# The causal mask's addition to the forget-gate rows: from DVE to an adding transfer of GpSimd, with another order of steps

## The chip, the cores and the metric

The kernel runs on one core of a Trainium2 chip. The metric is the device time of one launch in microseconds (us); the time before is the median of three runs. Five engines work side by side, each through its own queue in the order in which the program was written: TensorE (PE: matrix products and transposes), VectorE (DVE), ScalarE (ACT), GpSimd (POOL) and SyncE (SP, which here only starts transfers). A DMA started by SP or POOL stands in that engine's queue like any other instruction.

## What is computed

Two layers of a decoder over 512 tokens with 1024 features. Each layer has a mixing stage (three token mixers beside each other on one projection), a gated MLP and a small gated embedding stage. The part the change is about is the third mixer, attention with a forget gate, 6 heads of 64, in blocks of 128 queries:

```
c = jnp.cumsum(log_f, axis=1)                 # one row of 512 per head
s = einsum(q_i, k) * scale + c_i[..., None] - cT[:, :, None, :]
s = where(key_pos[None, :] <= q_pos[:, None], s, -inf)
out = softmax(s) @ v
```

So each score needs the key's running gate sum, and the diagonal block of 128x128 of each query block also the causal mask. The other two mixers are spatial gating (SGU) and retention (6 heads, with rotary position encoding); all three are put side by side and multiplied with `w_o`.

## The kernel before

Every instruction is first recorded by `Plan.record` and then issued in an order that `Plan.issue` (L452) works out, so all rows of the profile carry L452, and work is known by its tile. The planner models the engines, follows the order of recording as priority, and lets each stage's weight preparation run ahead of its use by a limit in the table `AHEAD` (L62). The order on each engine is therefore a result of the planner, of `AHEAD`, and of the order of steps in `STEPS` (L494): `u`, `s` are the spatial gating, `F` the attention's values and gate sums (`fox_values`, L1014), `H` the combined halves of the activations (`hT.combine`), `f0` to `f2` the query and key projections of three pairs of heads (`fox_proj`, L1052), `a0` to `a2` the attention of these pairs (`fox_attend`, L1066), `r0` to `r2`, `v`, `c0` to `c2` retention's projections, values and cores, `g`, `G`, `L` its gates. `O_ORDER` (L497) is the order in which `out_proj` (L1220) takes the eight 128-row blocks of the concatenation; blocks 5 to 7 are the three pairs of attention heads, 2 to 4 the retention.

The projections (`seven`, L860) multiply 2x2 blocks with seven products instead of eight. `seven_weights` (L837) prepares their weights: SP loads the tile `graw`, POOL starts two adding transfers into it (L847, L848), DVE makes two more sums, and ACT and DVE split each into a rounded part and a rest (`wg`, `wu`, `wsa`, `wsb`). Each exact product is three products on PE (`mm3`, L908).

In a layer the gate sums of six heads are made on PE (`cumps`, transposed as `ctps`), and written by SP as six rows to memory (`cums`). `fox_proj` takes one tile `fcb` (128x2048) for a pair of heads. For each head SP loads the row `cums`, broadcast to 128 partitions, as `cb[:, 0]`, and DVE writes `cb[:, 1]`, the same plus the mask. `fox_attend` reads `cb[:, 0]` for the blocks left of the diagonal and `cb[:, 1]` for the diagonal one, with a custom DVE instruction (`pe<-sps,fcb`) that adds the row to the scores and takes a minimum. ACT makes the exponential, DVE divides, PE transposes (`tps`, copied out as `fet` by DVE or ACT in turn), and PE multiplies with the values (`ops`), which ACT and DVE split into `cc` for `out_proj`.

Other names below: `ps<-thl,hT` are products of retention's values (`rv`, weights `traw` split into `thl`), `rm`, `rr` its rotated projections, `kps` transposes of the rotated key, `ips`, `rops`, `kvps` its core, `wo` the products of `out_proj`, `beta`, `alpha`, `gamma` the accumulators of `seven`, `hh`, `hhd`, `hT` its activations. `sps` is used by the attention scores and by the spatial gating. The mask before was a 128x128 tile in a slice of a larger tile (`mix`, L952), loaded once per layer (64 KB, L955).

Of the kernel before, what the change touches and what calls it, by code (L numbers as in the profile page):

```python
# [33 lines left out]
ALU = mybir.AluOpType  # L34
AX = mybir.AxisListType

P = 128
D = 1024
S = 512
NCH = 4  # L40
# [10 lines left out]
class Plan:  # L51
# [7 lines left out]

    SETS = {"X": 17, "W": 7}  # L60

    AHEAD = {"mix": 416, "wo": 450, "wo2": 381, "emb": 503, "gu0": 443, "gu": 478, "dn": 673, "end": 164, "pg": 300, "pg2": 392}  # L62
    LOAD = 1290
    TICK = 10240 / 3
    PHASE = 1900
# [186 lines left out]
    def issue(self):  # L252
# [41 lines left out]
        def blocked(i):  # L294
# [3 lines left out]
            for t in dict.fromkeys(ops[i][5]):  # L298
                if t not in taken:
                    tag, bufs = self.tiles[t][:2]  # L300
                    s = first[t]
                    need[tag] += 1
                    if len(slots[tag]) < need[tag] or s - front > self.AHEAD[self.stages[i]] or (s > front and live[tag][front:s].max() + need[tag] > bufs):
                        return queue(t)
# [4 lines left out]
        def queue(t):  # L309
            return f"b8 {self.kind[t]}" if t in self.kind else self.tiles[t][0]  # L310
# [160 lines left out]
def constants():  # L471
    idx = np.arange(P, dtype=np.float64)
    lg = np.log(1.0 - 2.0 ** (-5.0 - np.arange(6, dtype=np.float64)))
    diff = idx[None, :] - idx[:, None]
    decay = np.where(diff >= 0, np.exp(lg[:, None, None] * np.maximum(diff, 0.0)), 0.0) / 8.0
    qdec = np.exp(lg[:, None] * (idx + 1.0))
    kdec = np.exp(lg[:, None] * (P - 1.0 - idx)) / 8.0
    cd = np.exp(lg * P)
    hf = np.repeat(np.arange(2), 64)
    c = {}  # L480
    c["ident"] = np.eye(P)
    c["decay"] = decay.transpose(1, 0, 2).reshape(P, 6 * P)
    c["qdec"] = np.stack([qdec[2 * p + hf] for p in range(3)], 1).reshape(P, 3 * P)
    c["kdec"] = kdec.T
    c["cd"] = np.stack([cd[2 * p + hf] for p in range(3)], 1)
    c["invf"] = (10000.0 ** (-np.arange(32, dtype=np.float64) / 32))[np.arange(P) % 32][:, None]
    c["cum"] = np.concatenate([(idx[:, None] <= idx[None, :]).astype(np.float64), np.ones((P, P))], 1)
    c["mask"] = np.where(idx[None, :] <= idx[:, None], 0.0, 1e30)
    return {k: np.ascontiguousarray(v.astype(np.float32)) for k, v in c.items()}

PAIRS = [(c + p * P, d + p * P) for c, d in ((C_RQ, C_RK), (C_FK, C_FQ)) for p in range(3)] + [(C_RG, C_RG + P)]
STEPS = "u F H f0 g f1 r0 a0 v a1 G L s r1 r2 c0 f2 c1 c2 a2"  # L494
O_CHUNKS = (0, 2, 1, 3)
EARLY = {0: 0}
O_ORDER = (5, 6, 0, 1, 2, 3, 4, 7)  # L497
IDLE = 16
SUMS_BY_DMA = True
SEVEN = ("hb11", "hb21", "hh6", "hhd", "hh7", "hb22", "hh4")  # L500
# [2 lines left out]
def packed(w):  # L503

    def rows(m, order=None):

        m = m.reshape(-1, P, m.shape[-1])
        return (m if order is None else m[list(order)]).transpose(1, 0, 2)
# [16 lines left out]
    r["dn"] = [m.reshape(8, 4, P, 2, 512).transpose(0, 3, 2, 1, 4) for m in w["w_down"]]  # L525
    r["wo"] = [np.stack([rows(m[:, c:c + 512], O_ORDER) for c in (0, 512)]) for m in w["w_o"]]
    r["pg"] = [np.stack([rows(m[:, c:c + 512]) for c in (0, 512)]) for m in w["w_ple_gate"]]
# [4 lines left out]
def body(ctx, tc, a, out):  # L532
    nc = tc.nc
    plan = Plan(tc)
    V, A, G, T, SY = (plan.engine(n, e) for n, e in (
        ("DVE", nc.vector), ("ACT", nc.scalar), ("POOL", nc.gpsimd), ("PE", nc.tensor), ("SP", nc.sync)))
# [16 lines left out]
    def bank(name="ps"):  # L553
        return ppt([P, 512], F32, tag="ps", name=name, bufs=8)

    def wk(name, shape=(P, 512), dt=F32):
        return kpt(list(shape), dt, tag="wk", name=name, bufs=12)

    def b8(name, shape, dt=F32):
        kind = "W" if name in ("wg", "wsa", "wsb") else "X" if dt == F32R else None  # L560
        return b8t([P] + list(shape), dt, name, kind)
# [4 lines left out]
    def dram(name, shape):  # L566
        return dpt(list(shape), F32, tag=name, name=name, bufs=1)
# [96 lines left out]
    def v4(ps):  # L664
        return ps.rearrange("p (k t) -> p k t", k=4)
# [194 lines left out]
    def seven(h, ws, gs, us, scale=1.0, between=None):  # L860

        wg, wu, sa, sb = ws
        be, al, ga = (bank(n)[:, 0:256] for n in ("beta", "alpha", "gamma"))
        t1, t2 = slice(0, 256), slice(256, 512)

        def product(ps, w, n, first, last, part=range(4)):
            for k in part:
                ks = slice(k * P, k * P + P)
                mm3(ps, lambda i: w[i][:, ks], lambda i: h.part(n, i, k), first and k == 0, last and k == 3, True)

        def part(t, i):
            return [t[:, j, i * 512:i * 512 + 512] for j in range(2)]
        product(be, part(wg, 0), "b11", True, False)
        A.copy(gs[:, t1], be)
        product(al, part(wg, 1), "b21", True, True)
        V.tensor_tensor(out=gs[:, t1], in0=al, in1=gs[:, t1], op=ALU.add)
        product(be, part(sa, 0), "h6", False, False)
        A.copy(gs[:, t2], be)
        product(ga, part(sa, 1), "hd", True, False)
        if scale == 1.0:  # L880
            A.copy(us[:, t2], ga)
        else:
            A.mul(us[:, t2], ga, -scale)
        product(be, part(sb, 0), "h7", False, False)
        V.scalar_tensor_tensor(out=us[:, t2], in0=be, scalar=-scale, in1=us[:, t2], op0=ALU.mult, op1=ALU.subtract if scale == 1.0 else ALU.add)
        product(ga, part(sb, 1), "b22", False, True)
        V.tensor_tensor(out=gs[:, t2], in0=ga, in1=gs[:, t2], op=ALU.add)
        rest = between() if between else None
        product(be, wu, "h4", False, True, range(1) if rest else range(4))
        if rest:  # L890
            rest()
            product(be, wu, "h4", False, True, range(1, 4))
        A.mul(us[:, t1], be, -scale)
# [25 lines left out]
    def tm_chunk_major(act, u, n, done, order=range(KB), chunks=range(NCH)):  # L919
        for c in chunks:  # L920
            ps = bank()
            for j, k in enumerate(order):
                tm_mm(ps[:, 0:n], act, k, c, u, j == 0, j == KB - 1, 0, n, j)
            done(c, ps)
# [13 lines left out]
    cums = [[dram(f"cums{l}_{h}", (1, S)) for h in range(6)] for l in range(DEPTH)]  # L938


    def mixers(l, hT, uv, ready):
        plan.stage = "mix"
        m1, m2, m3, m4, m5, m6 = (b8(f"mix{i}", (2048,)) for i in range(6))
# [5 lines left out]
        au = m4[:, 0:1024].rearrange("p (c n) -> p c n", c=NCH)  # L949
        av = m4[:, 1024:2048].rearrange("p (c n) -> p c n", c=NCH)  # L950
        cst = m5[0:6, 0:512]
        mask = m5[:, 512:640]  # L952
        cosT = m5[:, 1536:2048]
        decay, qdec, cum, sinT = m6[:, 0:768], m6[:, 768:1152], m6[:, 1152:1408], m6[:, 1408:1920]
        for t, n in ((decay, "decay"), (qdec, "qdec"), (cum, "cum"), (mask, "mask")):  # L955
            SY.dma_start(out=t, in_=a["c_" + n])
        if l:
            SY.dma_start(out=sinT, in_=trig[:, 0, :])
# [93 lines left out]
        def fox_proj(p):  # L1052


            k, q = wk("fqk"), wk("fqk")
            seven(hT, seven_weights(a["w_fm"][l, 3 + p]), k, q, -0.125)
            tiles = [q, k]
            both = b8("fcb", (4, S))
            for s in range(2):
                cb = both[:, 2 * s:2 * s + 2, :]  # L1060
                SY.dma_start(out=cb[:, 0, :], in_=cums[l][2 * p + s].to_broadcast([P, S]))
                V.tensor_tensor(out=v4(cb[:, 1, :]), in0=v4(cb[:, 0, :]), in1=mask.unsqueeze(1).to_broadcast([P, NCH, P]), op=ALU.add)
                tiles.append(cb)
            return tiles

# [113 lines left out]
        fq, rq = {}, {}  # L1179
        for step in STEPS.split():  # L1180
            h = int(step[1]) if len(step) > 1 else 0
# [38 lines left out]
    def out_proj(l, cc, ready, x, new, g, nxt):  # L1220
# [4 lines left out]
        first = [bank("wo0") for _ in range(NCH)]  # L1225
        for j, k in enumerate(O_ORDER):
            for c in range(NCH):
# [18 lines left out]
        seen = []  # L1246
        tm_chunk_major(cc, u, 512, done, O_ORDER, O_CHUNKS)
        return emb
# [209 lines left out]
    g = Gains(None, ("mix_pre_g", 0))  # L1458
# [33 lines left out]
    for l in range(DEPTH):  # L1492
        ready = {}
        cc = mixers(l, hT, uv, ready)
        g = Gains(("mix_post_g", l), ("ffn_pre_g", l))
        hs = Seven(g)
        emb = out_proj(l, cc, ready, Rows(src), xd[3 * l], g, hs)
        g = Gains(("ffn_post_g", l), ("ple_pre_g", l))
        hT = Plain(g)
        ffn(l, hs, emb, ready, Rows(xd[3 * l]), xd[3 * l + 1], g, hT)  # L1500
        last = l + 1 == DEPTH
        g = Gains(("ple_post_g", l), None if last else ("mix_pre_g", l + 1))
        if last:
            ple(l, hT, Rows(xd[3 * l + 1]), ov, g, None)
        else:
            nxt = Mixed(g)
            ple(l, hT, Rows(xd[3 * l + 1]), xd[3 * l + 2], g, nxt)
            hT, src = nxt, xd[3 * l + 2]
            uv = tm_units(a["w_uv"][l + 1], 512)
# [24 lines left out]
```

## Time and profile before

| | us |
| --- | --- |
| runs, median of 3 | 1566.68 (1566.16 to 1568.85) |
| profiled execution | 1566.79 |
| its span in the profile | 1564.8 |
| PE busy | 1546.8 (99%) |
| DVE busy | 1219.5 (78%) |
| ACT busy | 888.6 (57%) |
| POOL busy | 193.3 (12%) |

The granted clock of PE was 0.998 of full speed. In a row of the timeline the first number is the start from the beginning of the span, the second the time to the modelled end of the last instruction merged into it, and a bracket gives the idle time of the engine just before and what ended it. Because PE's instructions are pipelined, the ends of one row and the start of the next overlap; the time of a run of products is best read from start to start. From the timeline, the mixing stage of layer 0 runs from about 44 to 215 us of the span and that of layer 1 from about 745 to 985; MLP and embedding fill the rest.

### The profile page before, as it was taken

What the parts mean: (1) busy time and instruction counts of PE and PEld (TensorE: products, weight loads), DVE (VectorE), ACT (ScalarE), POOL (GpSimd) and SP (SyncE); (2) the same over time, 40 slices, a digit from 0 to 9 for tenths busy, and PEclk for the clock granted to TensorE, in tenths of its full rate; (3) what the DMA queues carried; (4) which work ended last, traced back from release to release, by engine and by line L of the source; (5) the groups of instructions that cost most, each with busy time, mean ns of one, the idle gap of its engine ahead of it and who ended that gap; (6) DMA issues with size and microseconds to landing.
All of it is one profiled execution on the core that took longest, in us unless ns stands there. A gap on an engine that the chain in (4) does not pass through costs nothing.

```text
span 1564.8 us, 26898 instructions
## 1 busy us (share of the span) xinstructions
PE 1546.8 (99%) x10554; PEld 1401.3 (90%) x10554; DVE 1219.5 (78%) x2036; ACT 888.6 (57%) x1501; POOL 193.3 (12%) x233
## 2 busy tenths in 40 slices
PE   9999999999999999999999999999999999999997
PEld 6998878999899999998889898799999999999986
DVE  6778978977778778767796789799677788687685
ACT  8556647765554545535584576586555455455362
POOL 1111112101101111000120101121101011011010
PEclk9999999999999999999999999999999999999999
DMA  9444529545637446456474346295546455455641
GB/s 331 92 123 104 180 90 291 134 121 142 169 81 198 137 96 176 130 156 247 155 216 102 85 122 210 76 301 136 145 112 155 143 136 147 128 150 148 232 158 54
DMA packets 87877, 239.00 MB, mean 153 GB/s; under 512 B 10036, under 2 KB 18364, under 8 KB 87752
## 3 DMA queue, kind: packets, MB, share of 16 engines
q1 hardware_dynamic: 64856, 195.81, 36.0%
q0 software_dynamic: 22464, 40.90, 16.4%
q8 instruction: 82, 1.34, 0.3%
q10 hardware_dynamic: 432, 0.59, 0.1%
q14 instruction: 43, 0.35, 0.1%
HBM read 219.94 MB, written 17.33 MB: 152 GB/s over the span
## 4 chain that ended last, share of the span: by engine, by line
PE 91%; ACT 3%; DMA 3%; DVE 2%; issue 1%; SPq 0%; POOLq 0%; POOL 0%; DVEq 0%; ACTq 0%
PE beta L452 26%; PE dn L452 21%; PE ps L452 14%; PE gamma L452 13%; PE alpha L452 6%; PE wo L452 3%; DMA graw<-in_w_gu_dram 2%; PE hps L452 1%; PE sps L452 1%; PE tps L452 1%; PE ops L452 1%; PE eps L452 1%; PE gps L452 1%; ACT thl L452 1%; PE rops L452 1%
## 5 line engine op out<-in xcount | busy, mean ns | idle before, releaser
L452 PE MATMUL dn<-thl,act 128*128 128x512 f32 x1536 | 370.5, 391 | 0.0
L452 PEld LDWEIGHTS dn<-thl,act 128*128 128x128 f32 x1536 | 280.4, 188 | 52.3
L452 PE MATMUL ps<-thl,hT 128*128 128x512 f32 (+3 forms) x984 | 209.7, 368 | 1.1 <-ACT hT L452 0.9
L452 POOL DMA_DIRECT2D graw<-in_w_gu_dram x128 | 112.4, 917 | 759.0 <-DVE wg L452 162.2
L452 PEld LDWEIGHTS ps<-thl,hT 128*128 128x128 f32 x984 | 175.1, 188 | 25.0 <-ACT hT L452 1.5
L452 DVE TENSOR_TENSOR thl<-traw,thl 128x1024 fp32r<-128x1024 f32 (+3 forms) x124 | 142.3, 1155 | 19.3 <-ACT thl L452 19.2
L452 ACT CAST thl<-traw 128x1024 fp32r<-128x1024 f32 (+3 forms) x124 | 121.3, 995 | 22.0 <-DVE wsb L452 8.9
L452 PEld LDWEIGHTS beta<-hh,wu 128*128 128x128 f32 x936 | 125.6, 188 | 9.1
L452 PE MATMUL beta<-hh,wu 128*128 128x256 f32 x936 | 130.2, 279 | 0.0
L452 PE MATMUL beta<-hh,wsa 128*128 128x256 f32 x936 | 122.0, 279 | 1.2 <-ACT gs L452 0.8
L452 PE MATMUL beta<-hh,wsb 128*128 128x256 f32 x936 | 120.5, 278 | 2.0 <-ACT gs L452 1.5
L452 PE MATMUL gamma<-hhd,wsa 128*128 128x256 f32 x936 | 121.7, 278 | 0.0
L452 DVE TENSOR_TENSOR wsb<-graw,wsb 128x1024 fp32r<-128x1024 f32 x78 | 95.3, 1222 | 29.5 <-PE beta L452 16.8
L452 PEld LDWEIGHTS beta<-hh,wsa 128*128 128x128 f32 x936 | 113.4, 188 | 2.6 <-ACT gs L452 1.4
L452 PEld LDWEIGHTS beta<-hh,wsb 128*128 128x128 f32 x936 | 112.9, 188 | 2.8 <-ACT gs L452 2.1
L452 DVE TENSOR_TENSOR graw<-graw 128x512 f32<-128x512 f32 x156 | 106.3, 686 | 10.8 <-DMA graw<-in_w_gu_dram 8.3
L452 PEld LDWEIGHTS gamma<-hhd,wsa 128*128 128x128 f32 x936 | 113.8, 188 | 0.0
L452 DVE TENSOR_TENSOR facc<-dn,facc 128x512 f32<-128x512 f32 x112 | 77.0, 687 | 45.1 <-PE dn L452 44.8
L452 DVE TENSOR_TENSOR wg<-graw,wg 128x1024 fp32r<-128x1024 f32 x78 | 95.2, 1220 | 15.8 <-ACT wg L452 8.7
L452 DVE TENSOR_TENSOR wsa<-graw,wsa 128x1024 fp32r<-128x1024 f32 x78 | 95.2, 1220 | 14.7 <-ACT wsa L452 14.6
L452 PE MATMUL beta<-hb,wg 128*128 128x256 f32 x768 | 100.5, 278 | 1.3 <-DVE hb L452 0.8
L452 DVE SCALAR_TENSOR_TENSOR cv<-gs,cw,cv 128x511 f32<-128x511 f32 (+1 forms) x128 | 95.3, 745 | 7.5 <-ACT cv L452 7.1
(225 smaller groups left out, 2625.4 us busy)
## 6 DMA issues: line engine op xcount, KB each, us to landing
graw<-in_w_gu_dram SPq DMA_DIRECT2D x128, 512.0 KB
graw<-in_w_gu_dram POOLq DMA_DIRECT2D x128, 256.0 KB, 5.4
traw<-in_w_dn_dram SPq DMA_DIRECT2D x64, 512.0 KB
x<-x SPq DMA_DIRECT2D x40, 512.0 KB
graw<-in_w_fm_dram SPq DMA_DIRECT2D x28, 512.0 KB
traw<-in_w_wo_dram SPq DMA_DIRECT2D x16, 512.0 KB
traw<-in_w_pg_dram SPq DMA_DIRECT2D x16, 512.0 KB
graw<-in_w_fm_dram POOLq DMA_DIRECT2D x28, 256.0 KB, 4.7
```

What stands on the lines that cost most here:

```text
L452: made = o[1](*[self.map(v) for v in o[2]], **{k: self.map(v) for k, v in o[3].items()})
```

## The change

The mask's constant becomes 128x512 (the 128x128 mask four times beside each other), stays in memory, and is no longer loaded as a tile. In `fox_proj`, `cb[:, 1]` is a second broadcast load of the same row by SP, and POOL then starts a transfer that reads the mask (256 KB) and adds it to `cb[:, 1]`. The twelve DVE instructions that added the mask (6 heads in 2 layers) and the two mask loads are gone; twelve loads of 256 KB on SP and twelve adding transfers of 256 KB on POOL are new. Beside that the table of limits, the order of steps and the last two entries of the block order of `out_proj` change:

```
-    AHEAD = {"mix": 416, "wo": 450, "wo2": 381, "emb": 503, "gu0": 443, "gu": 478, "dn": 673, "end": 164, "pg": 300, "pg2": 392}
+    AHEAD = {"mix": 416, "wo": 445, "wo2": 399, "emb": 567, "gu0": 432, "gu": 478, "dn": 3000, "end": 184, "pg": 203, "pg2": 619}
...
-    c["mask"] = np.where(idx[None, :] <= idx[:, None], 0.0, 1e30)
+    c["mask"] = np.tile(np.where(idx[None, :] <= idx[:, None], 0.0, 1e30), (1, NCH))
...
-STEPS = "u F H f0 g f1 r0 a0 v a1 G L s r1 r2 c0 f2 c1 c2 a2"
+STEPS = "u H F g f0 f1 r0 a0 v a1 G L s r2 r1 c0 f2 c1 a2 c2"
...
-O_ORDER = (5, 6, 0, 1, 2, 3, 4, 7)
+O_ORDER = (5, 6, 0, 1, 2, 3, 7, 4)
...
-        mask = m5[:, 512:640]
...
-        for t, n in ((decay, "decay"), (qdec, "qdec"), (cum, "cum"), (mask, "mask")):
+        for t, n in ((decay, "decay"), (qdec, "qdec"), (cum, "cum")):
...
-                SY.dma_start(out=cb[:, 0, :], in_=cums[l][2 * p + s].to_broadcast([P, S]))
-                V.tensor_tensor(out=v4(cb[:, 1, :]), in0=v4(cb[:, 0, :]), in1=mask.unsqueeze(1).to_broadcast([P, NCH, P]), op=ALU.add)
+                for i in range(2):
+                    SY.dma_start(out=cb[:, i, :], in_=cums[l][2 * p + s].to_broadcast([P, S]))
+                G.dma_start(out=cb[:, 1, :], in_=a["c_mask"], accum_op=ALU.add)
```

What the planner makes of it is read from the order of instructions on each engine. The order of the MLP on PE and SP is as before; it differs in the mixing stages. Three places follow.

On PE, layer 0, from the last scores of the first query blocks of the first pair of heads on; before:

```order
L452 MATMUL sps<-fqk 128x512 x2
L452 MATMUL ps<-thl,hT 128x384 x12
L452 MATMUL tps<-k_ident,pe 128x128
L452 MATMUL ps<-thl,hT 128x384 x14
L452 MATMUL tps<-k_ident,pe 128x128
```

and now:

```order
L452 MATMUL sps<-fqk 128x512 x2
L452 MATMUL ps<-thl,hT 128x384 x31
L452 MATMUL tps<-k_ident,pe 128x128
L452 MATMUL ps<-thl,hT 128x384 x5
L452 MATMUL tps<-k_ident,pe 128x128
```

The first transpose of attention probabilities stood behind 12 products of the values and the second behind 14 more; now 31 stand ahead of the first. In layer 1 it was 15 and 17, and is 29 ahead of the first.

On PE, layer 0, in the retention core; before:

```order
L452 MATMUL beta<-hh_509,wu 128x256 x12
L452 MATMUL kps<-k_ident,rm 128x128 x2
L452 MATMUL rops<-mix_1112,inn 128x64 x2
L452 MATMUL rops<-R,qd 128x128
L452 MATMUL rops<-mix_1112,inn 128x64 x2
L452 MATMUL rops<-R,qd 128x128
L452 MATMUL rops<-mix_1112,inn 128x64 x2
L452 MATMUL rops<-R,qd 128x128
L452 MATMUL rops<-mix_1112,inn 128x64 x2
L452 MATMUL kps<-k_ident,rm 128x128
L452 MATMUL sps<-fqk 128x128 x2
```

and now:

```order
L452 MATMUL beta<-hh_497,wu 128x256 x12
L452 MATMUL sps<-fqk 128x384 x2
L452 MATMUL ips<-rm 128x128 x8
L452 MATMUL kps<-k_ident,rm 128x128 x3
L452 MATMUL wo_2055<-thl,cc 128x512
L452 MATMUL rops<-mix_1115,inn 128x64 x2
L452 MATMUL rops<-R,qd 128x128
```

The transposes `kps` stand together now, where one stood alone between products of the core and scores. Over the whole order the passages from unrounded fp32 products (`sps`, `ips`, `kvps`, `rops`, `ops`, `cumps`) straight to a transpose, or back, fall from 20 to 6; the passages from and to the rounded products stay as many.

On POOL, at the start of layer 1's mixing stage; before:

```order
L452 TENSOR_TENSOR rs<-vh,minus_half 128x1
L452 DMA graw<-in_w_fm_dram 128x512 x7
L452 TENSOR_TENSOR y<-vh,minus_half 128x16
L452 AFFINE_SELECT sguw<-sguw 128x512
L452 DMA graw<-in_w_fm_dram 128x512 x3
```

and now:

```order
L452 TENSOR_TENSOR rs<-vh,minus_half 128x1
L452 DMA graw<-in_w_fm_dram 128x512 x6
L452 DMA fcb<-in_c_mask_dram 128x512
L452 DMA graw<-in_w_fm_dram 128x512
L452 DMA fcb<-in_c_mask_dram 128x512 x3
L452 TENSOR_TENSOR y<-vh,minus_half 128x16
L452 AFFINE_SELECT sguw<-sguw 128x512
L452 DMA graw<-in_w_fm_dram 128x512 x3
```

The adding transfers of the mask stand among those of the weights: one weight sum (the second of the unit `r0`, retention's first pair) is behind the first of them, and `y`, the factor of the spatial gating's norm, behind all four. In layer 0 all weight sums issued before `a0` stay ahead of the mask's. On SP the loads of retention's values stand behind eight loads of `fcb` instead of four in either layer. At the end of the mix the last attention products (`ops` of the third pair) move closer to their use: of the `wo` products 8 (layer 0) and 6 (layer 1) stand between them and the first that needs block 7; before it was 21.

## Rows read from the trace of the kernel before

**Rows 1.** Page: busy us, share of the span and instructions of each engine.

```profile
PE 1546.8 (99%) x10554; PEld 1401.3 (90%) x10554; DVE 1219.5 (78%) x2036; ACT 888.6 (57%) x1501; POOL 193.3 (12%) x233
```

**Rows 2.** Windows of both mixing stages: length, busy per engine, clock, DMA share, GB/s.

```profile
60.00:160.00 100.00, 98.74 (x742) 89.70 (x740) 79.91 (x206) 61.43 (x119) 11.34 (x12) 1.00 0.40 104
160.00:215.00 55.00, 54.68 (x409) 45.41 (x410) 49.51 (x124) 31.29 (x57) 7.76 (x9) 1.00 0.49 163
...
828.00:930.00 102.00, 101.98 (x772) 93.94 (x771) 78.56 (x206) 61.28 (x117) 11.12 (x12) 1.00 0.39 103
930.00:985.00 55.00, 54.48 (x399) 44.70 (x399) 49.75 (x125) 32.74 (x61) 7.78 (x9) 1.00 0.51 172
```

**Rows 3.** PE timeline, layer 0, from the first values product; starts and durations in us.

```profile
103.96 2.35 PE L452 MATMUL ps<-thl,hT 128*128 128x384 f32 x12
...
106.18 2.70 PE L452 MATMUL ps<-thl,hT 128*128 128x384 f32 x14
110.02 0.33 PE L452 MATMUL tps<-k_ident,pe 128*128 128x128 f32 x1 [1.14 <-DVE fet L452]
```

**Rows 4.** DVE timeline of the same stretch.

```profile
108.47 0.69 DVE L452 TENSOR_TENSOR rm<-rm,mix 128x512 f32<-128x512 f32 x1 [1.58 <-ACT rr L452]
```

**Rows 5.** PE timeline, layer 1, the same place.

```profile
873.14 2.88 PE L452 MATMUL ps<-thl,hT 128*128 128x384 f32 x15
876.04 0.33 PE L452 MATMUL tps<-k_ident,pe 128*128 128x128 f32 x1
```

**Rows 6.** PE timeline, layer 0: transposes in a run of four, and one alone.

```profile
181.55 0.66 PE L452 MATMUL cps<-k_ident,ro 128*128 128x128 f32 x4
181.97 1.62 PE L452 MATMUL beta<-hh,wu 128*128 128x256 f32 x12
...
186.05 0.28 PE L452 MATMUL kps<-k_ident,rm 128*128 128x128 f32 x1
186.25 1.14 PE L452 MATMUL sps<-fqk 64*128 64x128 f32 x8
```

**Rows 7.** PE waits by tile, whole span: total us, times, longest.

```profile
PE beta L452 <- ACT fqk L452: 0.7, 2, 0.5
```

**Rows 8.** PE timeline: the same product in twelves, at two places of layer 0.

```profile
62.18 1.52 PE L452 MATMUL alpha<-hT,wg 128*128 128x256 f32 x12
...
73.09 1.58 PE L452 MATMUL alpha<-hT,wg 128*128 128x256 f32 x12
```

**Rows 9.** Tile fcb, whole span (duration ns min/median/max, first and last start).

```profile
L452 DVE TENSOR_TENSOR fcb<-fcb,mix x12: 680/684/693, 82.6 to 924.8; 128x512 f32<-128x512 f32 x12
```

**Rows 10.** DVE timeline, layer 0: fourth mask addition, last split of values' weights, first reader.

```profile
88.47 0.69 DVE L452 TENSOR_TENSOR fcb<-fcb,mix 128x512 f32<-128x512 f32 x1 [1.67 <-DMA fcb<-cums]
...
95.40 0.94 DVE L452 TENSOR_TENSOR thl<-traw,thl 128x768 fp32r<-128x768 f32 x1
...
102.12 0.29 DVE L452 CUSTOM_DVE_ANT_0 pe<-sps,fcb 128x128 f32<-128x128 f32 x1 [0.57 <-PE sps L452]
```

**Rows 11.** Page: adding transfers (q0: packets, MB, share), and their landing in us.

```profile
q0 software_dynamic: 22464, 40.90, 16.4%
...
graw<-in_w_fm_dram POOLq DMA_DIRECT2D x28, 256.0 KB, 4.7
```

**Rows 12.** PE, layer 0: `wo` products after the last attention products.

```profile
211.97 6.21 PE L452 MATMUL wo<-thl,cc 128*128 128x512 f32 x26
```

**Rows 13.** ACT and DVE timeline, layer 0: the split of the first pair's attention output.

```profile
122.91 0.59 ACT L452 CAST cc<-ops 128x512 fp32r<-128x512 f32 x1 [2.01 <-PE ops L452]
...
123.53 0.69 DVE L452 TENSOR_TENSOR cc<-ops,cc 128x512 fp32r<-128x512 f32 x1 [3.83 <-ACT cc L452]
```

**Rows 14.** Layer 1, unit `r0`: its second weight sum (POOL), its reader (DVE), its product (PE).

```profile
842.49 0.86 POOL L452 DMA_DIRECT2D graw<-in_w_fm_dram x1 [0.63 <-DVE wg L452]
...
854.61 1.41 DVE L452 TENSOR_TENSOR graw<-graw 128x512 f32<-128x512 f32 x2
...
863.60 1.58 PE L452 MATMUL beta<-hh,wsa 128*128 128x256 f32 x12
```

## The prediction

> **What bounds the kernel now.** I read the page first: PE is busy 99% of the span [rows 1], and the granted clock is 1.00 in every stretch of both mixing stages [rows 2]. So a microsecond is won only where PE waits, or where PE's own work gets shorter; work taken from DVE counts only where PE waits for DVE. Then the windows, because the change moves work in the two mixing stages alone: in the four stretches PE idles 100.00 - 98.74 = 1.26, 0.32, 0.02 and 0.52 us, together 2.12 us [rows 2]. That is all the waiting there is to remove at these places. DVE is busy 80%, 90%, 77% and 90% of them [rows 2]: loaded, but with room. Then PE's timeline, for where these waits are. The largest is one of 1.14 us in layer 0, where PE stands ready for the second transpose of attention probabilities while DVE has not yet copied out the first [rows 3]; DVE itself had lost 1.58 us just before, waiting for ACT's rotated `rr` [rows 4]. The same place in layer 1 shows no wait [rows 5]. Two further waits of together 0.7 us are for ACT's `fqk`, both in the retention cores [rows 7]. No wait of PE is for `fcb` or the mask.
>
> **The mask, taken off DVE.** Twelve additions of 0.684 us go [rows 9], 8.2 us of DVE. On the path they are worth nothing by themselves. The fourth of layer 0 ends at 88.47 + 0.69 = 89.2, the first reader starts at 102.12, and that one waits for PE's scores [rows 10]. DVE loses its 1.67 us wait ahead of that fourth addition too [rows 10], again 13 us before anything there is used. What hides this edit is PE's stream; without that cover it would be worth up to 8.2 us. I take 0 directly; the relief of DVE enters in the term for the transpose wait below.
>
> **The mask, put on the transfers.** The 156 adding transfers of 256 KB that the kernel has took 16.4% of 16 engines' span [rows 11]: 0.164 x 1564.8 / 156 = 1.65 us of all sixteen each. At that price, which for a plain load is an upper bound, 12 loads and 12 adding transfers cost 24 x 1.65 = 39.5 us of the DMA engines. The share in these stretches is 0.39 to 0.51 [rows 2], so there is room. What counts is who is late. (a) The diagonal tile: its load, then the adding transfer (0.86 us to issue [rows 14], 4.7 to land [rows 11]) ends 5.6 us after the load. The load landed by 88.47, so about 94 against the reader's 102.12 [rows 10]: 8 us spare. (b) Retention's value weights, on SP behind eight loads in place of four: 4 x 1.65 = 6.6 us later at most. Their last split ended at 95.40 + 0.94 = 96.3 [rows 10], and the first product is at 103.96 [rows 3]: 7.6 us spare. (c) POOL's queue in layer 1: the second sum of `r0` stands behind the first mask addition, which waits for a load, and behind it stand further mask additions and then the spatial gating's `y`. The sum was issued at 842.49 and read at 854.61 [rows 14]. With a load that lands as an adding transfer does, it issues 4.7 + 0.86 later, at 848.1, and has landed at 852.8: 1.8 us before its reader. All three fit, (c) with least room, so I take 0, with both ends in the range: below nothing there is no reason for a gain, above it is the rival C.
>
> The Trainium skill ("DMA: Bandwidth & Descriptors", section "Issuing engines are not separate DMA queues") speaks against this edit: transfers started by SP and by POOL run on the same 16 DMA engines and interleave, so starting the mask from GpSimd gives it no bandwidth of its own. By that rule (b) and (c) are shared delays; with the spares from the rows the sum would be the same, and without them it would be the rival C's. The half-full DMA share is how far the trace bears on it.
>
> **The order: the transpose wait.** With the new order 31 products of the values stand ahead of the first transpose. One takes (876.04 - 873.14) / 15 = 0.19 us [rows 5], so 31 are 5.9 us, and with the five behind it the second transpose comes about 6.9 us after the first product. Before, it could start 110.02 - 103.96 = 6.1 us after it [rows 3]. So the wait closes with 0.8 us in hand: -1.14 us. The other end is 0: DVE's chain there hangs on ACT's `rr` [rows 4], and the order of the projections around it changes. I take -1.14, since in layer 1, with more products ahead, the wait was not there [rows 5].
>
> **The order: changes between kinds of work on PE.** Straight passages between unrounded fp32 products and transposes fall from 20 to 6. A transpose alone among such products took 186.25 - 186.05 = 0.20 us, one in a run of four (181.97 - 181.55) / 4 = 0.105 [rows 6]: 0.095 more. 14 fewer at 0.095 are -1.3 us. A lone transpose has two such passages, so the small end is 7 x 0.095 = -0.7; the large end, if each side of a passage loses as much, is -2.7. I take -1.3, nearest to what the rows show for each passage removed.
>
> **The order: other waits.** The 0.7 us for `fqk` [rows 7] sit where cores and projections interleave, which the new order rearranges; I give it half, -0.35, between 0 and -0.7. New waits can arise at the end of the mix: the last attention products are followed by 8 (layer 0) and 6 (layer 1) `wo` products before their result is needed. One takes 6.21 / 26 = 0.24 us [rows 12], so 1.9 and 1.4 us. The split took from 122.91 to 123.53 + 0.69 = 124.22, 1.3 us, when both engines were free [rows 13]. That just fits; if ACT or DVE is in a longer instruction then, as much as 1.4 us is late in each layer (a pair of weight sums on DVE is 1.41 [rows 14]). I take +0.4, between 0 and +2.8.
>
> **A spread that belongs to no edit.** The same twelve products took 1.52 us at one place and 1.58 at another [rows 8], 5 ns each, and the spacing changes at interruptions of the stream. A stretch of 300 products that changes its spacing is 1.5 us either way; I put no value on it, but it widens the range.
>
> **The sum**, against the profiled execution (span 1564.8, time 1566.79, 1.99 outside the span): 0 + 0 - 1.14 - 1.3 - 0.35 + 0.4 = -2.4, so a span of 1562.4 and a time of 1564.4. The profiled execution is 0.11 above the median of the runs, so 1564.3. Worst ends together (0, -0.7, 0, +2.8) give +2.1, best ends (-1.14, -2.7, -0.7, 0) give -4.5. Pairing all ends is unlikely; with the spread of spacing the forecast's own range is 1562.3 to 1566.3.
>
> **Rivals.**
> - B, a larger gain: every wait in the moved stretches goes and the changes of kind save their large end: -1.14 - 0.7 - 2.7 = -4.5, 1562.2. For it speaks that nothing new need arise and that DVE gains 8.2 us in stretches where it is 90% busy [rows 2]; against it, that such an order has its own near misses, as at the end of the mix.
> - C, slower, by the POOL queue in layer 1. If all eight loads and four mask additions go ahead of `r0`'s sum on the DMA engines, that is 12 x 1.65 = 19.7 us, then 4.7 for its own landing [rows 11], 1.41 for DVE's pair of sums and as much for the split [rows 14]: 27.2 us from 842.49, while the product stood at 863.60, 21.1 us later [rows 14]. That is 6 us late; with half of the twelve ahead it is 3.7 us early. It decides from nine of the twelve ahead (14.8 + 7.5 = 22.3). I price it between 1 and 6, +4: 1570.7. Against it: the sum needs only the first load, by its place on POOL.
> - D, a trade: the order gives back what it takes (new waits of 2.8 us in place of the kinds and waits saved), and the mask was never on the path: 0, so 1566.7. For it speaks that the mixing stages had only 2.12 us of waits left [rows 2], so that any new one cancels quickly.
>
> The Trainium skill ("SBUF — State Buffer", section "SBUF: two separate sides") describes one more way to C: descriptors of a GpSimd transfer are held up while DVE runs an instruction in a two-port mode. By that rule a mask addition started beside dense DVE work would be late by such instructions, and the time would go toward C. The trace does not show it: a POOL issue took 0.86 us while DVE worked on splits [rows 14].
>
> **Chances and range.** The forecast 0.50, B 0.30, D 0.12, C 0.08. About 0.2%, 3.1 us, is what a measurement of this kernel can tell from no change, so faster means below 1563.5, slower above 1569.8. The forecast's range lies about a quarter below 1563.5 (0.13) and B about four fifths (0.24): faster 0.38. Slower takes most of C and a little of the rest, 0.09. Same 0.53. The range takes in B with a spread of 1.3 below it and D with as much above it: 1560.9 to 1568.0; what is left out is C and the tails.
>
> **What would show it.** In the profile after: no wait of `tps` on `fet` near 110 us (right), or one of another name in that stretch (D). `kps` transposes in threes with the next product about 0.1 us per transpose later (1.3), or still 0.2 (none). `wo` waiting for `cc` near 210 and 980 us would be the new wait, above 1 us each the worse end. `graw` or `beta<-hh,wsa` waiting for a transfer near 860 us is C. `pe<-sps,fcb` waiting for a DMA ahead of 102 us would overturn (a). What would make the prediction wrong as a whole is a change of spacing in long streams of products outside the mixing stages, or a new wait at the layer's start, where the combined halves `hh` now come ahead of the value weights' splits on DVE.

## The result: slower by 0.3%

| | before | after |
| --- | --- | --- |
| median of 14 runs | 1567.27 us | 1571.68 us |
| range of the runs | 1564.36 to 1569.30 | 1569.03 to 1575.08 |
| ratio after / before, 95% interval | | 1.0030 (1.0022 to 1.0038) |
| profiled execution, span | 1566.79, 1564.8 | 1569.03, 1567.3 |

The change costs 4.4 us; 1564.3 was forecast, and the range ended at 1568.0. The profiled execution of after is the fastest of its 14, so its span understates the loss. The windows of both mixing stages of after (columns as in [rows 2]):

```profile
60.00:160.00 100.00, 99.00 (x752) 90.84 (x752) 73.51 (x198) 60.05 (x116) 16.26 (x18) 1.00 0.54 127
160.00:215.00 55.00, 52.61 (x394) 43.46 (x395) 52.07 (x126) 33.03 (x60) 8.35 (x9) 1.00 0.51 178
...
828.00:930.00 102.00, 100.90 (x770) 92.50 (x769) 70.36 (x195) 59.09 (x114) 15.48 (x17) 1.00 0.51 126
930.00:985.00 55.00, 52.80 (x384) 43.62 (x385) 51.68 (x126) 33.05 (x61) 7.72 (x8) 1.00 0.52 184
```

PE idles 1.00, 2.39, 1.10 and 2.20 us in them, together 6.7 where it was 2.1. PE's waits by tile over the whole span of after show new names:

```profile
PE beta L452 <- ACT rm L452: 3.3, 4, 1.0
...
PE rops L452 <- DVE inn L452: 1.1, 2, 0.6
...
PE tps L452 <- DVE nm L452: 0.8, 2, 0.4
PE rops L452 <- DVE R L452: 0.6, 2, 0.3
PE beta L452 <- DVE rm L452: 0.3, 1, 0.3
```

None of them was there before. `tps` on `fet` (1.14) and `fqk` (0.7, [rows 7]) are gone. The new waits stand at two kinds of place.

**The layer starts.** First PE, then ACT, then SP in layer 0 of after, timelines:

```profile
92.93 1.58 PE L452 MATMUL alpha<-hT,wg 128*128 128x256 f32 x12
95.39 1.68 PE L452 MATMUL beta<-hh,wsa 128*128 128x256 f32 x12 [0.89 <-ACT rm L452]
```

```profile
93.96 0.83 ACT L452 CAST thl<-traw 128x768 fp32r<-128x768 f32 x1 [5.16 <-DMA traw<-in_w_rv_dram]
94.70 0.38 ACT L452 ACTIVATE fqk<-beta 128x256 f32<-128x256 f32 x1
94.97 0.36 ACT L452 COPY rm<-beta 128x256 f32<-128x256 f32 x1
```

```profile
73.75 12.63 SPq L452 DMA_DIRECT2D fcb<-cums  x8
86.42 4.76 SPq L452 DMA_DIRECT2D traw<-in_w_rv_dram  x4
```

PE waits for a copy out of its accumulator (`rm<-beta`). The product that it reads had ended at about 93, but ACT executes its queue in order, and ahead of it stands the cast of the value weights, which waits 5.16 us for its load. That load was issued behind eight loads of `fcb`. The same happens in layer 1 (0.99 us at 864.95). The windows from 75 to 100 us of before and of after show why the load takes so long:

```profile
75.00:100.00 25.00, 25.00 (x214) 24.91 (x213) 18.91 (x28) 12.41 (x21) 3.89 (x3) 1.00 0.60 161
```

```profile
75.00:100.00 25.00, 24.11 (x206) 23.91 (x205) 13.67 (x21) 11.33 (x22) 4.37 (x5) 1.00 0.95 232
```

The DMA share (second last column) was 0.60 there and is 0.95: full.

**The retention cores.** PE in layer 0 of after, the rows with a wait; in layer 1 four of the five recur with the same lengths:

```profile
161.79 1.63 PE L452 MATMUL beta<-hh,wsa 128*128 128x256 f32 x12 [0.71 <-ACT rm L452]
...
167.58 1.65 PE L452 MATMUL beta<-hh,wu 128*128 128x256 f32 x12 [0.30 <-DVE rm L452]
...
187.32 0.66 PE L452 MATMUL rops<-mix,inn 128*128 128x64 f32 x4 [0.57 <-DVE inn L452]
...
192.31 0.66 PE L452 MATMUL rops<-mix,inn 128*128 128x64 f32 x4 [0.28 <-DVE R L452]
...
197.99 0.30 PE L452 MATMUL tps<-k_ident,pe 128*128 128x128 f32 x1 [0.40 <-DVE nm L452]
```

Together 2.3 us in layer 0 and 2.0 in layer 1. The first follows a row of eight rotation copies `rr` on ACT, 154.09 to 159.46, and two casts; in the order of before, the copy of `beta` stood ahead of the casts.

### The profile page after: what moved, and what is told of

Read it like the earlier page. It is cut to its first block, busy times and chain, and to the rows that moved or that the text cites. A ratio compares the mean times of both kernels' runs of the same rounds, so it can differ in the third digit from the quotient of the medians.

```text
span 1567.3 us, 26928 instructions
## 1 busy us (share of the span) xinstructions
PE 1545.6 (99%) x10554; PEld 1401.1 (89%) x10554; DVE 1212.5 (77%) x2024; ACT 887.7 (57%) x1501; POOL 205.2 (13%) x245
## 3 DMA queue, kind: packets, MB, share of 16 engines
q0 software_dynamic: 24192, 44.05, 17.6%
## 5 line engine op out<-in xcount | busy, mean ns | idle before, releaser
L452 ACT CAST wsa<-graw 128x1024 fp32r<-128x1024 f32 x78 | 81.8, 1049 | 36.9 <-DVE graw L452 15.0
```

The costliest lines, as they stand in the source:

```text
L452: made = o[1](*[self.map(v) for v in o[2]], **{k: self.map(v) for k, v in o[3].items()})
```

## Experiments

Two theories. TRANSFERS: the 24 new transfers make other loads late. ORDER: the new order of steps costs time whatever the mask does. In the tables below the ratio is to before, with its 95% interval.

### Four kernels in which the planner works anew

`mask_only` has the new mask with `AHEAD`, `STEPS` and `O_ORDER` of before; `order_only` the new tables with the mask on DVE. `old_tail` and `old_head` are the change with one half of the step order put back:

```
-STEPS = "u H F g f0 f1 r0 a0 v a1 G L s r2 r1 c0 f2 c1 a2 c2"
+STEPS = "u H F g f0 f1 r0 a0 v a1 G L s r1 r2 c0 f2 c1 c2 a2"     (old_tail)
+STEPS = "u F H f0 g f1 r0 a0 v a1 G L s r2 r1 c0 f2 c1 a2 c2"     (old_head)
```

> The changed mask (second load and adding transfer on GpSimd) with the step order, limits and block order of before. Theory ORDER (the loss comes from the new order: ACT's copies of the retention projections stand behind other work, 1.9 us at the two layer starts and 4.2 us in the two retention stretches): the ACT order here has both copies ahead of the casts of the value weights, so no wait of beta on ACT rm of 0.9 us, and a time within 1.5 us of before. Theory TRANSFERS (the 24 new transfers delay other loads): 4 to 5 us slower than before, as the whole change is.

> The step order, limits and block order of the change with the mask still added on DVE. Theory ORDER: the waits of the retention stretches (beta on ACT rm 0.7, rops on DVE inn 0.6 and on DVE R 0.3, tps on DVE nm 0.4, in each layer) stay, those at the layer starts shrink since the value weights' loads are issued earlier: 2 to 4 us slower than before. Theory TRANSFERS: within 1.5 us of before or up to 3 us faster, as the order alone was forecast.

> The whole change, but the second half of the step order as before (r1 r2 c0 f2 c1 c2 a2). Theory ORDER: the waits of the retention stretches go (about 4 us), those of 0.9 us at the two layer starts stay: between 0 and 2 us slower than before. Theory TRANSFERS: as slow as the whole change, 4 to 5 us.

> The whole change, but the first half of the step order as before (u F H f0 g). Theory ORDER: the two waits of 0.9 us at the layer starts go, since ACT has its copies ahead of the casts again; the retention waits stay: 2 to 3.5 us slower than before. Theory TRANSFERS: as slow as the whole change, 4 to 5 us.

| kernel | ratio | interval |
| --- | --- | --- |
| mask_only | 1.0084 | 1.0067 to 1.0100 |
| order_only | 1.0030 | 1.0019 to 1.0041 |
| old_tail | 1.0031 | 1.0020 to 1.0043 |
| old_head | 1.0050 | 1.0036 to 1.0064 |

Neither theory alone gives this: the mask alone costs 13 us, the tables alone 4.7, both together 4.4, and putting back either half of the steps helps nothing. The parts are not additive, and a kernel in which the planner works anew is not a change of one thing: the order on every engine comes out anew, the places of casts too. In `mask_only` the second cast of the value weights stands so late on ACT that PE waited for that instead (the largest new wait by tile):

```profile
PE ps L452 <- ACT thl L452: 3.2, 1, 3.2
```

At the end of this wait PE's granted clock fell (the last section has the numbers), so that part of the 13 us is a slower clock. So the next kernels hold the order fixed.

### The mask and the order apart, with fixed orders

Both kernels take the finished order of one version and exchange only what is issued at its places. `before_order_transfers`, written short:

```
-                SY.dma_start(out=cb[:, 0, :], in_=row)
-                V.tensor_tensor(out=cb[:, 1, :], in0=cb[:, 0, :], in1=mask, op=ALU.add)
+                SY.dma_start(out=cb[:, 0, :], in_=row); SY.dma_start(out=cb[:, 1, :], in_=row)
+                G.dma_start(out=cb[:, 1, :], in_=a["c_mask"], accum_op=ALU.add)
```

`after_order_dve` does the reverse in the order of the change (the mask tile in a free slice).

> Every instruction in the order of before, held fixed; only the twelve additions on DVE are left out, each first load of fcb is followed by the second one, and POOL starts the adding transfer at the place of the addition. It prices the transfers without any new order. Theory TRANSFERS (the DMA engines are full from about 75 to 100 us of the span and the loads of retention's value weights come late): 2 to 5 us slower than before, with PE waits near 95 to 110 us and 865 to 880 us for ACT's copies of rm or casts of thl. Theory ORDER (the loss is the new order): within 1 us of before.

> Every instruction in the order of the change, held fixed; the twelve second loads are left out and DVE adds the mask at the place of the adding transfers. It prices the order without the transfers. Theory ORDER: the waits of the retention stretches stay (about 2 us in each layer), less what the changes of kind save (1.3): 2 to 4 us slower than before. Theory TRANSFERS: the waits of beta on ACT rm at the layer starts go and the rest cancels: within 1 us of before, 3.5 to 5 us faster than the whole change.

| | mask on DVE | mask by transfers |
| --- | --- | --- |
| order of before | 1 | 1.0064 (1.0051 to 1.0076) |
| order of the change | 1.0014 (1.0005 to 1.0023) | 1.0030 (1.0022 to 1.0038) |

Now it adds up: the transfers cost 10 us in the old order and 2.5 in the new one, and the new order by itself costs 2.2. Each theory was half right. ORDER's 2 to 4 us holds the 2.2; TRANSFERS' 2 to 5 us was at most half of the 10. With a fixed order the starts of PE's rows can be laid side by side. The lengths of stretches, each worked out as the difference of two starts in PE's timeline (gate sums: start of the last `cumps`; first scores: first `sps<-fqk`; then first `ops`; then first `dn`):

| us | before | before_order_transfers | after_order_dve | after |
| --- | --- | --- | --- | --- |
| layer 0, gate sums to first scores | 30.67 | 36.55 | 31.65 | 32.80 |
| layer 1, the same | 33.11 | 36.64 | 33.28 | 34.13 |
| layer 0, first scores to first ops | 18.89 | 18.94 | 17.62 | 17.61 |
| layer 1, the same | 17.73 | 17.96 | 17.28 | 17.35 |
| layer 0, first ops to first dn | 181.82 | 181.90 | 183.60 | 183.75 |
| layer 1, the same | 185.43 | 185.07 | 187.37 | 187.26 |

Between two columns of one order only the mask differs. There the first two lines hold the transfers' price and no other does: 5.88 + 3.53 = 9.4 us in the old order, 1.15 + 0.85 = 2.0 in the new one. The last two hold the order's: 1.78 + 1.94 = 3.7 us lost, against 1.27 + 0.45 = 1.7 won on the way to the first `ops`. (From before to `after_order_dve` the first line also holds a shift: the gate sums start at 69.16 in place of 70.23, and the 0.98 us are that.) Between the two orders the last two stretches do not hold quite the same work: PE issues 1276 and 1301 products in them before and 1277 and 1303 in `after_order_dve` and after, since three products of the values have moved behind the first `ops`. At 0.19 us each [rows 5] that is 0.6 us, so the real loss is about 3.1 and the real gain about 1.1. PE's busy time in the windows of `after_order_dve` that begin and end at these starts is 179.56 + 184.79 = 364.35; before it is 179.70 + 184.50 = 364.20. Its idle time there rose from 3.05 to 6.62 us. So the loss is waiting.

In the old order nearly all of the cost at layer 0's start is one wait. PE, then ACT, of `before_order_transfers`:

```profile
99.02 2.70 PE L452 MATMUL beta<-hh,wsa 128*128 128x256 f32 x12 [4.41 <-ACT rm L452]
```

```profile
94.19 0.83 ACT L452 CAST thl<-traw 128x768 fp32r<-128x768 f32 x1 [5.29 <-DMA traw<-in_w_rv_dram]
94.93 1.04 ACT L452 CAST wsb<-graw 128x1024 fp32r<-128x1024 f32 x1
96.05 0.83 ACT L452 CAST thl<-traw 128x768 fp32r<-128x768 f32 x1
97.59 0.83 ACT L452 CAST thl<-traw 128x768 fp32r<-128x768 f32 x1 [0.71 <-DMA traw<-in_w_rv_dram]
98.33 0.38 ACT L452 ACTIVATE fqk<-beta 128x256 f32<-128x256 f32 x1
98.60 0.36 ACT L452 COPY rm<-beta 128x256 f32<-128x256 f32 x1
```

Three casts of the value weights stand ahead of the copy here, one in the change: this is why the new order pays less for the same lateness. In layer 1 the same two steps hold ACT's copies of `fqk`, behind casts that waited 4.62 and 2.08 us for their loads, and with them PE (this kernel):

```profile
865.39 1.65 PE L452 MATMUL beta<-hh,wsb 128*128 128x256 f32 x12 [1.95 <-ACT fqk L452]
868.59 1.63 PE L452 MATMUL gamma<-hT,wsb 128*128 128x256 f32 x12 [1.55 <-ACT fqk L452]
```

Together they are 3.5 us, the whole of the 3.53 in the table.

### What holds PE at the layer start

`copies_first` is the change with two casts of the value weights in each layer moved behind the first two copies of `rm`. In layer 0 ACT's order, shortened, becomes:

```
-CAST thl, COPY rm<-beta, CAST thl, COPY rm<-beta
+COPY rm<-beta, CAST thl, COPY rm<-beta, CAST thl
```

> The whole change with one exchange on ACT in each layer: the copies of the first retention projection (rm) stand ahead of the casts of the value weights that wait for their loads, all else in the order of the change. If those casts hold the copies and these hold PE (the waits of 0.9 and 1.0 us): 1.5 to 2 us faster than the change, about 2.5 us slower than before. If PE then waits for the value weights themselves instead: no faster than the change.

1.0039 (1.0026 to 1.0051): no faster than the change. In layer 0 ACT served both copies in time, and then the third one, `rm<-gamma`, stood behind the next waiting cast (PE and ACT of this kernel):

```profile
99.82 1.65 PE L464 MATMUL gamma<-hT,wsb 128*128 128x256 f32 x12 [0.97 <-ACT rm L464]
```

```profile
98.66 0.83 ACT L464 CAST thl<-traw 128x768 fp32r<-128x768 f32 x1 [0.77 <-DMA traw<-in_w_rv_dram]
99.40 0.36 ACT L464 COPY rm<-gamma 128x256 f32<-128x256 f32 x1
```

The wait only moved. In layer 1, where more casts stand between the copies, the second copy still came behind three of them, and PE waited 0.66 us for it in place of 0.99 for the first. So the late load has to go, not one place behind it. `second_pair_late` (the change) and `before_pair_late` (the order of before with the transfers) move the four `fcb` loads and two adding transfers of the second pair of heads behind the loads of the value weights (names written out):

```
+        early = [j for j in order[:order.index(last_rv_load)] if j in second_pair_transfers]
+        order = [j for j in order if j not in early]
+        at = order.index(last_rv_load) + 1
+        order[at:at] = early
```

> The whole change with the four fcb loads and two adding transfers of the second pair of heads moved behind the loads of the value weights in each layer, all else in the order of the change. If the full DMA engines make the value weights late: the casts start 3 to 5 us earlier, the waits of beta on ACT rm at the layer starts go, 1.5 to 2 us faster than the change. If the queue of loads is not what makes them late: no difference.

> The order of before with the transfers, as in the kernel that cost 9 us, but the four fcb loads and two adding transfers of the second pair of heads behind the loads of the value weights in each layer. If the value weights that wait behind these loads carry the cost: most of it goes, 1 to 4 us slower than before in place of 9. If the transfers cost by sheer amount wherever they stand: 8 to 10 us slower as there.

| kernel | ratio | interval | without the move |
| --- | --- | --- | --- |
| second_pair_late | 1.0019 | 1.0009 to 1.0028 | 1.0030 |
| before_pair_late | 0.9996 | 0.9987 to 1.0005 | 1.0064 |

The second line settles it for the order of before: the same 24 transfers cost 10 us when those of the second pair of heads stand ahead of the value weights' loads, and nothing that can be told when they stand behind. The first four loads of `fcb` (two heads) may stay ahead. SP and ACT of `before_pair_late`, then its window and the same window of `before_order_transfers`:

```profile
76.19 1.77 SPq L1078 DMA_DIRECT2D fcb<-cums  x4
78.05 7.39 SPq L458 DMA_DIRECT2D traw<-in_w_rv_dram  x4
85.64 2.86 SPq L1078 DMA_DIRECT2D fcb<-cums  x4
```

```profile
89.04 0.83 ACT L458 CAST thl<-traw 128x768 fp32r<-128x768 f32 x1
```

```profile
75.00:100.00 25.00, 24.72 (x218) 24.52 (x217) 16.80 (x24) 12.85 (x21) 6.88 (x7) 1.00 0.89 232
```

```profile
75.00:100.00 25.00, 20.59 (x172) 20.39 (x171) 13.74 (x19) 11.12 (x18) 4.36 (x5) 0.99 0.84 226
```

The cast no longer waits, though the DMA share is 0.89, above the 0.84 of the kernel that lost 10 us. So a high share alone did not cost the time here; what mattered is which load comes last. The Trainium skill ("DMA: Bandwidth & Descriptors", section "Issuing engines are not separate DMA queues") says that transfers of all issuing engines share the DMA engines and interleave. The trace is in line with it: in `second_pair_late` DVE waited 2.79 us for a weight sum that POOL had issued at 74.90, while SP's loads of `fcb` and of the value weights ran.

`second_pair_late` gained 1.7 us of the 2.5 by the medians, but its interval overlaps that of the change; its trace shows the gain: the waits for ACT's `rm` at both layer starts are gone, and the first two stretches of the table are 32.25 and 33.11 in place of 32.80 and 34.13. It is now as far from before as `after_order_dve` within the intervals; what is left is mainly the order's own loss. In layer 0 it has a new wait of 1.21 us (`beta` on DVE's `wsa`), since that weight sum was late.

### The retention cores

`turn_on_pool` is `after_order_dve` with half of the rotation copies of both late projections on POOL (in effect; their places in the order stay):

```
-                    A.copy(r[s + 32:s + 64, :], m[s:s + 32, :])
+                    (G.tensor_copy if p else A.copy)(r[s + 32:s + 64, :], m[s:s + 32, :])
```

> The order of the change with the mask on DVE, as in the kernel that cost 1.5 to 2 us, and half of the row of eight rotation copies (rr) that ACT does in a stretch in both late retention projections is done by POOL. If this row on ACT is what makes the copy of beta into rm late (PE waits of 0.7 us in each layer): these waits go, about 1.5 us less, within 1 us of before. If DVE's splits set the end of that wait: no change; if POOL's copies are slow (over 1 us each), slower.

1.0015 (1.0006 to 1.0024), the same as without it. The wait on ACT's `rm` is gone, but DVE's are in its place (PE's waits by tile, this kernel):

```profile
PE wo L452 <- DVE inn L452: 2.3, 2, 1.2
...
PE beta L452 <- DVE wsa L452: 1.6, 2, 0.8
```

POOL's copies took 0.9 us each (four from 153.05 in 3.75), against ACT's 0.62. While they ran, DVE's additions and products of the same shape took up to 1.09 us in place of 0.69 (DVE, first of this kernel, then of `after_order_dve`):

```profile
155.23 1.09 DVE L452 TENSOR_TENSOR rm<-rm,mix 128x512 f32<-128x512 f32 x1
```

```profile
159.61 1.22 DVE L452 TENSOR_TENSOR wsa<-graw,wsa 128x1024 fp32r<-128x1024 f32 x1
```

The second row says why relieving ACT gained nothing there: without the POOL copies DVE's split of `wsa` ended at 159.61 + 1.22 = 160.83, as late as ACT's copy (160.65). With them ACT's copy was done at 158.75, but DVE, slowed beside POOL, ended the split at 160.93. So ACT's row was not the only thing late; how much DVE would have gained from a faster ACT without POOL's copies, this kernel does not tell. That stays open, as does which of the exchanges (`r2 r1`, `a2 c2`) makes which wait. That the copy of `beta` stands behind the two casts was not tested by itself either.

### Two tries at something faster

`head_dve` is before with the first half of the new step order; the planner places the rest. `fet_first` is before with one exchange on DVE, the copy of the first transposed probabilities ahead of the two rotation products that [rows 4] shows waiting (its lines below are DVE's order, not code).

```
-STEPS = "u F H f0 g f1 r0 a0 v a1 G L s r1 r2 c0 f2 c1 c2 a2"
+STEPS = "u H F g f0 f1 r0 a0 v a1 G L s r1 r2 c0 f2 c1 c2 a2"     (head_dve)

-TENSOR_TENSOR rm<-rm,mix; TENSOR_TENSOR rr<-rr,mix; COPY fet<-tps
+COPY fet<-tps; TENSOR_TENSOR rm<-rm,mix; TENSOR_TENSOR rr<-rr,mix  (fet_first)
```

> The kernel before with the first half of the new step order alone (u H F g f0), mask on DVE, limits and second half as before; the planner places the rest anew. The first transpose of the probabilities still stands behind 12 products, so if that place decides there is no gain: within 1.5 us of before. If the new first half is what is wrong with the new order: 1 to 3 us slower.

> The kernel before with one exchange on DVE in layer 0: the copy of the first transposed probabilities stands ahead of the two rotation products (rm, rr) that wait for ACT. By the profile of before PE's wait of 1.14 us goes: 1 us faster than before, which is less than 0.1%. If DVE then holds the next copy instead: no change.

`head_dve`: 1.0045 (1.0033 to 1.0058), slower than any figure expected of it. By its profile the loss is in layer 1: from the last `cumps` to the first `dn` it took 242.99 us there in place of 236.27, in layer 0 231.46 in place of 231.38. The stretch from the first scores to the first `ops` took 21.69 in place of 17.73, though it holds fewer products: transposes waited four times, two of them for DVE's `pe`, and the granted clock fell (last section). `fet_first`: 1.0001 (0.9992 to 1.0010). The wait of 1.14 us went, and the next transpose waited 0.88:

```profile
108.15 0.27 PE L459 MATMUL tps<-k_ident,pe 128*128 128x128 f32 x1
...
110.89 0.41 PE L459 MATMUL tps<-k_ident,pe 128*128 128x128 f32 x2 [0.88 <-DVE pe L459]
```

No kernel of these beats before by more than its interval.

## Why the prediction was wrong

- **The mask off DVE, 0.** Right. DVE's busy time fell from 1219.5 to 1212.5 us. In `before_order_transfers`, which takes the mask off DVE and keeps the order, PE still waited 1.19 us for `fet` (1.14 before).
- **Price of the transfers.** Right in size. The adding transfers took 17.6% of 1567.3 us for 168, 1.64 us each. Loads: (0.367 x 1567.3 - 0.360 x 1564.8) / 12 = 0.99 us each, under the bound of 1.65. The average share of 0.40 over 100 us, however, said nothing of the 25 us in which the transfers stand; there the share was 0.60, and four loads and four adding transfers at these prices are 10.5 us of 25, another 0.42. This window should have been read.
- **(a), the diagonal tile.** Right: no reader of `fcb` waited for a DMA, though the fourth adding transfer of layer 0 was issued only at 93.60, when it was to have landed at about 94.
- **(b), the value weights: the step that failed for the transfers.** The lateness was inside its bound (the first cast at 93.96 in place of 89.54, 4.4 us; bound 6.6), and PE never waited for the value weights in after, as the 7.6 us spare said. But it took the product that uses the weights as the only one who waits. The instruction that waits is ACT's cast, and ACT's copies out of PE's accumulators are queued behind it. ACT before, layer 0:

```profile
89.54 0.84 ACT L452 CAST thl<-traw 128x768 fp32r<-128x768 f32 x1 [0.80 <-DMA traw<-in_w_rv_dram]
...
93.23 0.38 ACT L452 COPY rm<-beta 128x256 f32<-128x256 f32 x1
```

The cast already waited 0.80 us for its load, so it had no spare time at all, and the copy ended 0.83 us before the product that waits for it (94.44): not 7.6 us. `before_pair_late` shows that this step carries the whole cost of the transfers in the old order; in the new one the waits for ACT's `rm` at the layer starts (0.89 and 0.99) are most of the 2.0 us. The transfers, put at 0, cost 2.0 to 2.5 us. The last line of the prediction names a new wait at the layer's start as a sign of being wrong, but by way of DVE's splits, and gives it no price.

- **(c) and rival C.** C had the sign and nearly the time (1570.7), but that was luck: no wait of PE at `r0` is for a weight sum on POOL; PE's wait there (0.99, 864.95) is again for ACT's copy. Nor did POOL's issues of the mask get long: 0.88 us in the median of twelve. The sum itself came later than (c) had it: issued at 850.02 in place of 848.1, and not landed by 852.8 (DVE, layer 1 of after):

```profile
858.20 0.69 DVE L452 TENSOR_TENSOR graw<-graw 128x512 f32<-128x512 f32 x1 [3.60 <-DMA graw<-in_w_fm_dram]
```

DVE took up this wait: its split `wsa` ended at 861.31, 3.6 us before the product.

- **The transpose wait, -1.14.** Right. The wait is gone. The stretch from the first scores to the first `ops` is 1.28 us shorter in layer 0, of which one product that moved out of it is 0.19; the 0.38 in layer 1 are two such products and no gain.
- **Changes of kind, -1.3.** Not shown, either way. PE's busy time in the last two stretches was 364.35 against 364.20, with three products more (0.6 us), so PE may have saved about 0.4 us. But in `before_pair_late`, with PE's order as before, the first of these stretches had a busy time of 178.70 in place of 179.70: a spread as large as the term.
- **`fqk` -0.35 and new waits +0.4: the step that failed for the order.** The `fqk` waits went (0.7), and the end of the mix, which I named as the place of new waits, has none: `wo` follows `ops` without a bracket. But the cores, which I knew to be rearranged and gave no new wait, got waits of 2.3 and 2.0 us for `rm`, `inn`, `R` and `nm`. I costed the places where I had found a tight spot and gave the rest nothing, in stretches where DVE was 90% busy [rows 2] and PE waited almost nowhere. An order under which PE waits 0.8 us in two stretches of 55 can hardly get better and can easily get worse.

With measured terms the sum is -1.7 on the way to the first `ops` plus 3.7 for the rest of the mix (with the moved products in both) plus 2.0 for the transfers: 4.0, against the measured 4.4.

## What to carry to other kernels

A load that comes later costs the engine that waits for it everything queued behind that instruction, so ask what stands behind the waiting instruction before asking when its result is used. Read the DMA share in the window where new transfers will stand, not over the stage, and move those that are needed last behind those that another engine waits for: in the order of before that was the whole difference between 10 us and nothing. When an order is changed in a stretch where the bound engine waits almost nowhere, expect new waits in it, and keep an order fixed when two parts of such a change are to be told apart.

## What the runs showed of the hardware

PE's wait of 4.41 us in `before_order_transfers` cost more than itself. Its windows around it, and PE's rows behind the one that waited:

```profile
95.00:100.00 5.00, 0.98 (x5) 0.98 (x6) 4.33 (x5) 4.21 (x8) 0.00 (x0) 0.93 1.10 302
100.00:105.00 5.00, 5.00 (x35) 5.00 (x34) 2.32 (x4) 1.49 (x4) 3.21 (x2) 0.73 0.36 86
```

```profile
101.52 2.11 PE L452 MATMUL gamma<-hhd,wsa 128*128 128x256 f32 x12
103.46 1.52 PE L452 MATMUL beta<-hh,wsb 128*128 128x256 f32 x12
```

The granted clock (third number from the end) fell to 0.93 and 0.73, means of stretches at both levels (2.4 and 1.2 GHz), after PE had been idle; the twelve products after the wait took 2.50 us from start to start and the next twelve 1.94, where twelve took 1.41 just before the wait. These 1.09 and 0.53 us are why the stretch grew by 5.88 and not by 4.4. The clock fell also with waits of 2.67 us (`old_tail`, 0.84 and 0.81 from 95 to 100 and 100 to 105 us), 3.1 (`old_head`, 0.50 from 110 to 115) and 3.2 (`mask_only`, 0.66 from 110 to 115), and in `head_dve` after four waits of 0.49 to 0.73 us close together (0.87 and 0.79 from 880 to 885 and 885 to 890). The waits of about 1 us in after and those of 1.95 and 1.55 in layer 1 of `before_order_transfers` left it at 1.00.

The MLP, with PE's order unchanged, took from 436.9 to 439.0 us between its first and last `dn` in the profiles of before and after, layer by layer. One profile of each version therefore can't tell two microseconds; the stretches above could, since with a fixed order the untouched ones of the table agreed within 0.4 us. They are not always that steady: in `before_pair_late` layer 0's last stretch took 180.86 us, 0.96 less than before in the same order of PE.

DVE's instructions got longer beside POOL's copies: in `turn_on_pool` eight fp32 additions and products of 128x512 that ran beside them took 0.98 to 1.09 us, where the same shape takes 0.69 elsewhere in that kernel.
